# Layer norm's statistics partly on ScalarE, ReLU-squared wholly on ScalarE, and one more feature block ahead of each down projection, in a two-layer decoder trunk

## The chip, the cores and the metric

The kernel runs on one core of one Trainium2 chip. The time is that of one execution on the device, in microseconds (us); less is better. TensorE (PE) multiplies matrices, VectorE (DVE) and ScalarE (ACT) work element by element, GpSimd (POOL) takes a part of the subtractions, and SyncE (SP) issues the transfers. Each engine runs its instructions in the order in which they were written for it.

## The reference, cut to what matters

Two decoder layers over 512 rows of 1024 numbers in fp32. Layer 0 mixes with latent attention and windowed attention, layer 1 with forgetting attention. Each layer is

```
x = LN(alpha * x + mixer(x))                       # "ln1"
x = LN(alpha * x + square(relu(x @ w_up)) @ w_down) # "ln2"; w_up 1024x4096, w_down 4096x1024
x = x + sigmoid(x @ w_gate + b_gate) * (p @ w_proj)
LN(x) = (x - mean) * rsqrt(var + 1e-5) * g + b      # over the 1024 numbers of a row
```

## The kernel before, in words

**Tiling.** The rows are four blocks `tb` of 128. `x[tb][h]` is a tile of 128 rows by 512 columns, `h` being the half of the columns. PE needs its inputs split into a high part and a rest (`split`: ACT copies to the high part, DVE or POOL subtracts it), and each product is three matmuls (`mm3`). The transposed activations are the tiles `xh` and `xl`; `to_X` makes them from `x[tb]`: four transposes by PE for each half, then a split.

**Layer norms.** `out_proj` multiplies half 0 for all blocks and then half 1 block by block; after each bank DVE adds `ALPHA*x` (L1239), and after half 1 of a block `ln1` runs `layer_norm` and `to_X` for it. `down`, the end of the feed-forward part, does the same by block with `ln2` (residual sum L1352). `layer_norm` is DVE work alone: statistics of both halves (L1214), mean and variance (L1216), the square root's inverse by an integer start and three Newton steps on 128x1 columns (L1217, `rsqrt` L631 to L640), and two passes over each half (L1220, L1222).

**Feed-forward.** `up` makes one block of 128 of the 4096 features: 24 matmuls into one bank, then `relu2`, in which ACT takes the ReLU (L1259) and DVE multiplies it by the bank again (L1260), so the bank is free only after DVE. `up_first` makes the first four blocks in halves of 256 rows: the first half needs only row blocks 0 and 1. Features go in groups of four. `forms` turns a group into the seven sums and differences of a fast 2x2 product (splits and subtractions by ACT and DVE); `down_pairs` multiplies them by seven forms of the weights (tiles `wf`, made by `form`) into banks `t`, `mm` and `s`, and DVE adds each bank to `x` (L1330, L1332). PE's order is: one block of the next group, the products of this group, three more blocks.

**Order.** `Plan` lists every operation with an estimated duration and lays them out by engine: each engine takes the ready operation of the lowest number, and buffers come from rings of fixed depth (`DEPTH`; 12 tiles `w`, two for a plain weight, one for a form). That order is then fixed for each engine.

Of the kernel before, what the change touches and what calls it, by code (L numbers as in the profile page):

```python
# [93 lines left out]
def weight_pieces():  # L94
# [337 lines left out]
class Trunk:  # L432
# [194 lines left out]
    def rsqrt(self, y, v, r, w, n=1):  # L627
# [4 lines left out]
        d(lambda e: e.tensor_scalar(hv[:], v(), -0.5, None, ALU.mult), r, [hv])  # L632
        d(lambda e: e.tensor_scalar(y().bitcast(I32), y().bitcast(I32), -1, 0x5F3759DF, ALU.mult, ALU.add), [], [w])
# [573 lines left out]
        return [self.load("u", (P, 512), lambda h=h: self.A["rows"][i:i + 1, 512 * h:512 * h + 512].broadcast_to([P, 512]), name)  # L1207
                for h in range(2)]

    def layer_norm(self, x, g, b):  # L1210

        st, mv, rv = self.small("bn", 12), self.small("mv", 4), self.small("rv", 4)
        for h in range(2):
            self.dve(S, lambda e, h=h: e.bn_stats(st[:, 6 * h:6 * h + 6], x[h][:]), [x[h]], [(st, h)])  # L1214

        self.dve(1, lambda e: e.bn_aggr(mv[:, 0:2], st[:].rearrange("p (a b) -> p a b", a=2)), [st], [mv])  # L1216
        self.dve(1, lambda e: e.tensor_scalar(rv[:, 0:1], mv[:, 1:2], EPS, None, ALU.add), [mv], [(rv, 0)])  # L1217
        self.rsqrt(lambda: rv[:, 1:2], lambda: rv[:, 0:1], [(rv, 0)], (rv, 1))
        for h in range(2):
            self.dve(S + 57, lambda e, h=h: e.scalar_tensor_tensor(x[h][:], x[h][:], mv[:, 0:1], g[h][:], ALU.subtract, ALU.mult),  # L1220
                     [mv, g[h]], [x[h]], port=True)
            self.dve(S + 57, lambda e, h=h: e.scalar_tensor_tensor(x[h][:], x[h][:], rv[:, 1:2], b[h][:], ALU.mult, ALU.add),  # L1222
                     [(rv, 1), b[h]], [x[h]], port=True)

    def out_proj(self, x, order, after):
        xh, xl = self.X
        for h in range(2):
            ws = [self.weights() for _ in range(4)]
            banks = [None] * TB

            def step(tb, i):
                if i == 0:
                    banks[tb] = self.bank()
                ks = (2 * order[i], 2 * order[i] + 1)
                self.natural(banks[tb], 512, ws[i], tb, ks, i == 0, i == 3)
# [99 lines left out]
    def down(self, rl, x, after):  # L1335
# [3 lines left out]
            self.split(S, lambda a=a: a[:], lambda r=r: r[:, 0, :], lambda r=r: r[:, 1, :], [a], [r], psum=False)  # L1339
        ws = [self.weights() for _ in range(4)]  # L1340
        for tb in range(TB):
            ts = slice(tb * P, (tb + 1) * P)
            for h in range(2):
                cs = slice(512 * h, 512 * (h + 1))
                b = self.bank()
                for j in range(4):
                    r, w = rt[j], ws[j]
                    self.mm3(512, lambda b=b: b[:], (lambda r=r, ts=ts: r[:, 0, ts], lambda r=r, ts=ts: r[:, 1, ts]),
                             (lambda w=w, cs=cs: w[0][:, cs], lambda w=w, cs=cs: w[1][:, cs]), j == 0, j == 3,
                             [r] + list(w), [b])  # L1350
# [52 lines left out]
    def run(self):  # L1403
        A = self.A
        for l in range(2):
# [12 lines left out]
            def ln1(tb):  # L1418
                self.layer_norm(x[tb], g1, b1)
# [57 lines left out]
```

## Time and profile before

| | |
|---|---|
| three runs | 1271.53 us median (1270.67 to 1274.31) |
| the profiled execution | 1274.59 us, of which the span of instructions is 1272.8 us |
| busy: PE, DVE, ACT, POOL | 1237.7, 1008.5, 615.4, 503.2 us |
| TensorE's granted clock over the run | 0.995 of full speed |

The profile is of one execution. Its span runs from the first instruction to the last; 1.8 us lie around it. A row of the profile gives an engine, a line of the kernel and a tile; busy time counts an instruction from its start to its end, and neighbours on an engine overlap a little, so the step from one start to the next is shorter than a duration.

### The profile page before, as it was taken

What the parts mean: (1) busy time and instruction counts of PE and PEld (TensorE: products, weight loads), DVE (VectorE), ACT (ScalarE), POOL (GpSimd) and SP (SyncE); (2) the same over time, 40 slices, a digit from 0 to 9 for tenths busy, and PEclk for the clock granted to TensorE, in tenths of its full rate; (3) what the DMA queues carried; (4) which work ended last, traced back from release to release, by engine and by line L of the source; (5) the groups of instructions that cost most, each with busy time, mean ns of one, the idle gap of its engine ahead of it and who ended that gap; (6) DMA issues with size and microseconds to landing.
All of it is one profiled execution on the core that took longest, in us unless ns stands there. A gap on an engine that the chain in (4) does not pass through costs nothing.

```text
span 1272.8 us, 17267 instructions
## 1 busy us (share of the span) xinstructions
PE 1237.7 (97%) x6108; PEld 1044.7 (82%) x6108; DVE 1008.5 (79%) x1847; ACT 615.4 (48%) x1180; POOL 503.2 (40%) x408
## 2 busy tenths in 40 slices
PE   9998999999999999999999999999999999999998
PEld 6887888878888888888898888888788888888877
DVE  5668969799898999595543686878998998897774
ACT  6658852434444344334445697823444444444241
POOL 2445432445454444212213475422455444543110
PEclk9999999999999999999999999999999999999999
DMA  6422523124323222413222412531223242232131
GB/s 202 147 78 79 166 100 114 35 100 134 97 69 133 99 95 88 141 65 136 92 93 91 149 67 92 182 132 51 99 84 115 99 132 85 81 133 94 55 116 50
DMA packets 46791, 132.83 MB, mean 104 GB/s; under 512 B 5984, under 2 KB 8672, under 8 KB 46704
## 3 DMA queue, kind: packets, MB, share of 16 engines
q1 hardware_dynamic: 46704, 131.72, 31.0%
q8 instruction: 48, 0.79, 0.2%
q14 instruction: 39, 0.32, 0.1%
HBM read 126.03 MB, written 4.62 MB: 103 GB/s over the span
## 4 chain that ended last, share of the span: by engine, by line
PE 78%; DVE 13%; ACT 4%; issue 2%; DMA 2%; POOL 1%; SPq 0%; DVEq 0%; ACTq 0%; POOLq 0%
PE mm L512 30%; PE s L512 20%; PE t L512 15%; PE o L512 10%; PE t L523 2%; DVE wl L488 1%; DMA raw<-in_wall_dram 1%; DVE x L1220 1%; ACT t L664 1%; DVE x L1222 1%; DVE t L659 1%; DVE wf L488 1%; DVE xl L503 1%; DVE rl L503 1%; DVE qlo L753 1%
## 5 line engine op out<-in xcount | busy, mean ns | idle before, releaser
L488 POOL TENSOR_TENSOR wl<-raw,wh 128x1024 fp32r<-128x1024 f32 (+4 forms) x78 | 183.4, 2352 | 450.6 <-ACT wh L551 379.8
L551 ACT CAST wh<-raw 128x1024 fp32r<-128x1024 f32 (+5 forms) x150 | 151.8, 1018 | 195.3 <-DMA raw<-in_wall_dram 101.8
L488 POOL TENSOR_TENSOR wf<-raw,wf 128x512 fp32r<-128x512 f32 x84 | 124.5, 1503 | 128.2 <-ACT wf L584 128.2
L512 PE MATMUL mm<-xh,wh 128*128 128x512 f32 (+1 forms) x416 | 163.1, 392 | 1.9 <-DVE k L766 0.8
L512 PE MATMUL mm<-xl,wh 128*128 128x512 f32 (+1 forms) x416 | 160.7, 386 | 1.0 <-DVE xl L503 1.0
L512 PE MATMUL mm<-xh,wl 128*128 128x512 f32 (+1 forms) x416 | 160.3, 385 | 0.0
L584 ACT CAST wf<-raw 128x512 fp32r<-128x512 f32 x168 | 98.8, 619 | 32.0 <-PE t L512 16.6
L488 DVE TENSOR_TENSOR wl<-raw,wh 128x1024 fp32r<-128x1024 f32 (+4 forms) x72 | 95.7, 1329 | 21.1 <-ACT wh L551 18.4
L512 PE MATMUL t<-wf,rh 128*128 128x512 f32 x336 | 103.7, 390 | 0.0
L488 DVE TENSOR_TENSOR wf<-raw,wf 128x512 fp32r<-128x512 f32 x84 | 100.9, 1220 | 0.0
L673 POOL TENSOR_SCALAR t<-t,st 128x256 f32<-128x256 f32 (+3 forms) x128 | 69.4, 562 | 76.1 <-DVE st L670 52.7
L512 PEld LDWEIGHTS mm<-xh,wh 128*128 128x128 f32 x416 | 79.7, 192 | 19.3 <-ACT q L755 2.2
L512 PEld LDWEIGHTS mm<-xl,wh 128*128 128x128 f32 x416 | 79.8, 192 | 15.8 <-DVE xl L503 2.1
L512 PEld LDWEIGHTS mm<-xh,wl 128*128 128x128 f32 x416 | 79.6, 191 | 15.6 <-DVE wl L503 0.4
L512 PE MATMUL mm<-wh,xh 128*128 128x384 f32 (+5 forms) x232 | 82.8, 357 | 6.5 <-DVE qlo L753 2.7
L512 PE MATMUL mm<-wl,xh 128*128 128x384 f32 (+5 forms) x232 | 80.7, 348 | 0.2 <-POOL wl L488 0.2
L512 PE MATMUL mm<-wh,xl 128*128 128x384 f32 (+5 forms) x232 | 80.7, 348 | 0.0
L664 ACT ACTIVATE t<-t,st 128x256 f32<-128x256 f32 (+3 forms) x128 | 68.7, 539 | 13.0 <-DVE st L659 10.8
L512 PEld LDWEIGHTS t<-wf,rh 128*128 128x128 f32 x336 | 62.9, 188 | 13.7 <-DVE x L1330 0.7
L512 PE MATMUL s<-wf,rh 128*128 128x512 f32 x224 | 69.0, 389 | 0.0
L1332 DVE TENSOR_TENSOR x<-x,t 128x512 f32<-128x512 f32 x100 | 65.2, 677 | 1.4 <-PE t L512 1.3
L512 PE MATMUL t<-wf,rl 128*128 128x512 f32 x168 | 65.4, 389 | 0.0
(296 smaller groups left out, 3240.2 us busy)
## 6 DMA issues: line engine op xcount, KB each, us to landing
raw<-in_wall_dram SPq DMA_DIRECT2D x183, 512.0 KB, 3.3
ck<-scratch_c SPq DMA_DIRECT2D x16, 256.0 KB, 4.0
raw<-in_wall_dram SPq DMA_DIRECT2D x9, 384.0 KB, 3.1
x<-in_xT_dram SPq DMA_DIRECT2D x8, 256.0 KB, 5.4
x<-in_xn_dram SPq DMA_DIRECT2D x8, 256.0 KB, 4.9
g<-in_rows_dram SPq DMA_DIRECT2D x8, 256.0 KB, 4.7
b<-in_rows_dram SPq DMA_DIRECT2D x8, 256.0 KB, 6.3
scratch_x<-x SPq DMA_DIRECT2D x8, 256.0 KB, 2.3
```

What stands on the lines that cost most here:

```text
L488: fn = lambda e: e.tensor_tensor(out(), a(), b(), op)
L503: sub = lambda e: e.tensor_tensor(lo(), src(), hi().bitcast(F), ALU.subtract)
L512: return [self.nc.tensor.matmul(o(), a(), b(), start=s, stop=e, **kw) for o, a, b, s, e in prods]
L523: lambda: [self.nc.tensor.transpose(o(), i(), self.ident[:]) for o, i in items],
L551: self.act(w, lambda e: e.copy(hi[:, :w], raw[:, :w]), [raw], [hi])
L584: self.act(512, lambda e: e.copy(t[:, h[0]], src()), [key], [(t, 0)])
L659: return e.tensor_tensor_reduce(t[:, offs[i] + a:offs[i] + z], b[:, c + a:c + z], ad(), -scale, init, ALU.add, ALU.min, nm[:, i:i + 1])
L664: self.act(n, lambda e, i=i, tt=tt: e.activation(tt(), tt(), AF.Exp, bias=nm[:, i:i + 1], scale=-1.0, accum_out=sm[:, i:i + 1]), [(nm, i)] ...
L673: self.pool(0.13 + 1.21e-3 * n, lambda e, i=i, tt=tt: e.tensor_scalar(tt(), tt(), rc[:, i:i + 1], 1.0, ALU.mult, ALU.mult), [rc], [(t, i)])
L753: self.dve(S, lambda e, q2=q2, lo=lo, rs=rs: e.tensor_tensor(lo[rs, :], bank[rs, :], q2[rs, :].bitcast(F), ALU.subtract), [bank, (q2, 0)], ...
L1220: self.dve(S + 57, lambda e, h=h: e.scalar_tensor_tensor(x[h][:], x[h][:], mv[:, 0:1], g[h][:], ALU.subtract, ALU.mult), [mv, g[h]], [x[h] ...
L1332: self.dve(S, lambda e, b=b, xx=xx: e.tensor_tensor(xx[:], xx[:], b[:], ALU.add), [b], [xx])
```

## The change

- The row sum of the residual comes out of the same DVE instruction that adds it (`add_sum`, one column per half in a tile `st`). For `out_proj` ACT multiplies `x` by `ALPHA` ahead of that.
- `layer_norm`: DVE makes the negated mean from the two sums; ACT squares each half less the mean and sums it (bias and accumulator); DVE adds the two sums; ACT takes the square root; DVE takes its reciprocal and one Newton step. The two passes over each half stay.
- `relu2`: the square is an ACT instruction on the tile in SBUF, and DVE has no part in it.
- `ffn`: two blocks of the next group stand ahead of the products of this one, two behind; the weights are stored in that order.

```diff
-            up(range(4 * g + 4, 4 * g + 5) if g < 7 else ())
+            up(range(4 * g + 4, 4 * g + 6) if g < 7 else ())
...
-            up(range(4 * g + 5, 4 * g + 8) if g < 7 else ())
+            up(range(4 * g + 6, 4 * g + 8) if g < 7 else ())
...
+    def add_sum(self, xx, b, st, h):
+        self.dve(S + 26, lambda e: e.tensor_tensor_reduce(xx[:], b[:], xx[:], 1.0, 0.0, ALU.add, ALU.add, st[:, h:h + 1]),
+                 [b], [xx, (st, h)])
...
-    def layer_norm(self, x, g, b):
-        st, mv, rv = self.small("bn", 12), self.small("mv", 4), self.small("rv", 4)
-            self.dve(S, lambda e, h=h: e.bn_stats(st[:, 6 * h:6 * h + 6], x[h][:]), [x[h]], [(st, h)])
-        self.dve(1, lambda e: e.bn_aggr(mv[:, 0:2], st[:].rearrange("p (a b) -> p a b", a=2)), [st], [mv])
-        self.dve(1, lambda e: e.tensor_scalar(rv[:, 0:1], mv[:, 1:2], EPS, None, ALU.add), [mv], [(rv, 0)])
-        self.rsqrt(lambda: rv[:, 1:2], lambda: rv[:, 0:1], [(rv, 0)], (rv, 1))
...
+    def layer_norm(self, x, st, g, b):
+        d(lambda e: e.tensor_scalar(c(nm), st[:, 0:1], st[:, 1:2], -1.0 / D, ALU.add, ALU.mult), [st], [nm], 0.1)
+            self.act(S, lambda e, h=h, junk=junk: e.activation(junk[:], x[h][:], AF.Square, bias=c(nm), accum_out=q[:, h:h + 1]),
+                     [x[h], nm], [junk, (q, h)], aps=2)
...
+        d(lambda e: e.scalar_tensor_tensor(c(v), q[:, 0:1], D * EPS, q[:, 1:2], ALU.add, ALU.add), [q], [v], 0.1)
+        self.act(1, lambda e: e.activation(c(t), c(v), AF.Sqrt, scale=1.0 / D), [v], [t])
+        d(lambda e: e.reciprocal(c(y), c(t)), [t], [y], 0.1)
+        d(lambda e: e.tensor_scalar(c(hv), c(v), -0.5 / D, None, ALU.mult), [v], [hv])
+        d(lambda e: e.tensor_scalar(c(t), c(y), c(y), c(hv), ALU.mult, ALU.mult), [y, hv], [t], 0.19)
+        d(lambda e: e.scalar_tensor_tensor(c(y), c(t), 1.5, c(y), ALU.add, ALU.mult), [t], [y], 0.1)
...
+        for h in range(2):
+            for tb in range(TB):
+                self.act(S, lambda e, xx=x[tb][h]: e.mul(xx[:], xx[:], ALPHA), [], [x[tb][h]])
...
-                    self.dve(S, lambda e: e.scalar_tensor_tensor(xx[:], xx[:], ALPHA, b[:], ALU.mult, ALU.add), [b], [xx])
+                    self.add_sum(xx, b, sums[tb], h)
...
-            rl = [self.up()]
+            rl = [self.up() for _ in range(2)]
             self.down_pairs(g, rt, x)
-            rl += [self.up() for _ in range(3)]
+            rl += [self.up() for _ in range(2)]
...
-        self.dve(n, lambda e: e.scalar_tensor_tensor(rl[:, c0:c1], b[:, c0:c1], 0.0, rl[:, c0:c1], ALU.max, ALU.mult),
-                 [b], [(rl, c0)])
+        self.act(n, lambda e: e.activation(rl[:, c0:c1], rl[:, c0:c1], AF.Square), [], [(rl, c0)])
```

## Rows read from the trace of the kernel before

**Rows 1.** Busy time by stretch of the span: length; then PE, its weight loads (PEld), DVE, ACT and POOL with their instructions; TensorE's granted clock; DMA share and GB/s. 262:534 and 918:1186 are the feed-forward groups of the two layers, 534:582 is ln2 of layer 0.

```profile
262.00:534.00 272.00, 271.92 (x1199) 224.56 (x1198) 242.50 (x312) 117.13 (x193) 124.78 (x76) 1.00 0.32 107
534.00:582.00 48.00, 48.00 (x227) 39.66 (x226) 41.91 (x93) 17.40 (x26) 7.58 (x3) 1.00 0.23 81
...
918.00:1186.00 268.00, 268.00 (x1183) 221.97 (x1183) 237.85 (x307) 117.52 (x193) 122.34 (x73) 1.00 0.32 105
```

**Rows 2.** The same view in steps of 5 us through ln1 of layer 0.

```profile
205.00:210.00 5.00, 5.00 (x28) 4.24 (x27) 5.00 (x18) 1.44 (x2) 0.34 (x1) 1.00 0.00 2
...
215.00:220.00 5.00, 4.53 (x34) 3.92 (x33) 5.00 (x11) 2.38 (x4) 2.52 (x1) 1.00 0.32 107
...
230.00:235.00 5.00, 3.99 (x19) 3.22 (x20) 2.75 (x5) 1.17 (x2) 0.00 (x0) 0.72 0.00 0
```

**Rows 3.** The chain that ended last, in order of time: start, length, what. Layer 0's last halves of `up_first` and one undisturbed `up`, one half's transposes in ln2 of layer 0, the last `up_first` bank of layer 1.

```profile
242.84 2.89 PE s L512 x24
...
278.25 5.44 PE mm L512 x24
...
549.27 0.44 PE t L523 x4
...
894.46 2.89 PE o L512 x24
```

**Rows 4.** PE's instructions in order of time: start, duration, form, and in brackets the idle time before and what ended it. In layer 0 the first transposes of row block 0, the last matmul of `out_proj` and the first transposes of row block 3; then the last matmul of `out_proj` in layer 1.

```profile
208.57 0.60 PE L523 MATMUL s<-ident,x 128*128 128x128 f32 x4
...
213.32 0.39 PE L512 MATMUL s<-wh,xl 128*128 128x512 f32 x1
...
230.79 0.66 PE L523 MATMUL t<-ident,x 128*128 128x128 f32 x4 [1.59 <-DVE x L1222]
...
865.20 0.39 PE L512 MATMUL s<-wh,xl 128*128 128x512 f32 x1
```

**Rows 5.** Who waited for whom on PE over the whole run: us in total, times, the longest.

```profile
PE mm L512 <- DVE rl L1260: 3.4, 2, 1.7
...
PE mm L512 <- DVE x L1352: 0.7, 1, 0.7
PE mm L512 <- ACT pr L1373: 0.7, 1, 0.7
```

**Rows 6.** The chain again, DVE's pieces in ln1 of layer 0, row blocks 0 and 1.

```profile
201.02 0.22 DVE mv L1216
...
201.27 0.15 DVE rv L1217
201.42 0.66 DVE x L1220
202.08 0.06 DVE rv L631
202.14 0.06 DVE nh L632
...
202.78 0.14 DVE rv L633
202.93 0.59 DVE x L1239
203.52 0.19 DVE nt L636
203.71 0.60 DVE bn L1214
204.31 0.06 DVE rv L640
...
207.21 1.33 DVE x L1222 x2
```

**Rows 7.** DVE's and ACT's groups over the run by line and shape: count | busy us, mean ns of one | idle time before, and what ended it.

```profile
L1260 DVE SCALAR_TENSOR_TENSOR rl<-mm,rl 128x512 f32<-128x512 f32 x28 | 19.2, 686 | 10.1 <-ACT rl L1259 9.9
...
L659 DVE CUSTOM_DVE_ANT_0 t<-s,cmask 128x512 f32<-128x512 f32 x8 | 5.4, 681 | 0.0
...
L659 DVE DVE_READ_ACCUMULATOR2_ANT st<- 128x1 f32 x176 | 14.3, 81 | 0.0
...
L670 DVE RECIPROCAL st<-st 128x4 f32<-128x4 f32 x32 | 5.5, 173 | 6.8 <-ACT t L664 6.5
...
L664 ACT ACTIVATE t<-t,st 128x512 f32<-128x512 f32 x24 | 17.3, 719 | 2.6 <-DVE st L659 2.6
...
L664 ACT ACTIVATION_READ_ACCUMULATOR t<-t,st 128x1 f32 x128 | 24.4, 190 | 0.0
...
L668 ACT ACTIVATE st<-st,sinks 128x4 f32<-128x4 f32 x8 | 2.3, 289 | 0.0
...
L502 ACT ACT_TABLE_LOAD x1 | 1.3, 1283 | 0.7 <-PEq L1466 0.7
...
L1119 ACT ACT_TABLE_LOAD x1 | 1.3, 1283 | 0.0
```

**Rows 8.** ACT in order of time: the table load of layer 1 ahead of the logarithm (L1118) and the instruction after it; then ACT's longest idle time in ln1 of layer 0.

```profile
657.18 1.28 ACT L1118 ACT_TABLE_LOAD   x1
658.48 0.64 ACT L1118 ACTIVATE fl<-fw 16x512 f32<-16x512 f32 x1
...
208.53 1.05 ACT L551 CAST wh<-raw 128x1024 fp32r<-128x1024 f32 x1 [10.44 <-PE s L512]
```

More of the change, by code (lines that the diff above doesn't have):

```diff
@@ L625, in to_X, with rsqrt @@
                        lambda ks=ks: xl[:, ks, ts], [b], cells)
-    def rsqrt(self, y, v, r, w, n=1):
+    def rsqrt(self, y, v, r, w, n=1, scale=0):
         t, hv = self.small("nt", n), self.small("nh", n)
@@ L631, in rsqrt @@
         d(lambda e: e.tensor_scalar(y().bitcast(I32), v().bitcast(I32), 1, None, ALU.arith_shift_right), r, [w])
-        d(lambda e: e.tensor_scalar(hv[:], v(), -0.5, None, ALU.mult), r, [hv])
-        d(lambda e: e.tensor_scalar(y().bitcast(I32), y().bitcast(I32), -1, 0x5F3759DF, ALU.mult, ALU.add), [], [w])
+        d(lambda e: e.tensor_scalar(hv[:], v(), -0.5 / 4 ** scale, None, ALU.mult), r, [hv])
+        d(lambda e: e.tensor_scalar(y().bitcast(I32), y().bitcast(I32), -1, 0x5F3759DF + (scale << 23), ALU.mult, ALU.add), [], [w])
         for _ in range(3):
@@ L1208, in row @@
                 for h in range(2)]
-    def layer_norm(self, x, g, b):
-        st, mv, rv = self.small("bn", 12), self.small("mv", 4), self.small("rv", 4)
+    def add_sum(self, xx, b, st, h):
+        self.dve(S + 26, lambda e: e.tensor_tensor_reduce(xx[:], b[:], xx[:], 1.0, 0.0, ALU.add, ALU.add, st[:, h:h + 1]),
+                 [b], [xx, (st, h)])
+    def layer_norm(self, x, st, g, b):
+        nm, q, v, y = (self.small(n, 4) for n in ("nm", "sq", "va", "rs"))
+        c = lambda z: z[:, 0:1]
+        d = lambda fn, r, w, dur=0.07: self.dve(1, fn, r, w, dur=dur)
+        d(lambda e: e.tensor_scalar(c(nm), st[:, 0:1], st[:, 1:2], -1.0 / D, ALU.add, ALU.mult), [st], [nm], 0.1)
@@ L1213, in layer_norm @@
         for h in range(2):
[L1214 to L1218 removed]
+            junk = self.u("junk")
+            self.act(S, lambda e, h=h, junk=junk: e.activation(junk[:], x[h][:], AF.Square, bias=c(nm), accum_out=q[:, h:h + 1]),
+                     [x[h], nm], [junk, (q, h)], aps=2)
@@ L1219, in layer_norm @@
         for h in range(2):
[L1220 to L1223, printed above, removed]
+            self.dve(S + 57, lambda e, h=h: e.scalar_tensor_tensor(x[h][:], x[h][:], c(nm), g[h][:], ALU.add, ALU.mult),
+                     [nm, g[h]], [x[h]], port=True)
@@ new lines, in layer_norm @@
+        d(lambda e: e.scalar_tensor_tensor(c(v), q[:, 0:1], D * EPS, q[:, 1:2], ALU.add, ALU.add), [q], [v], 0.1)
+        hv, t = self.small("hv", 4), self.small("nt", 4)
+        self.act(1, lambda e: e.activation(c(t), c(v), AF.Sqrt, scale=1.0 / D), [v], [t])
+        d(lambda e: e.reciprocal(c(y), c(t)), [t], [y], 0.1)
+        d(lambda e: e.tensor_scalar(c(hv), c(v), -0.5 / D, None, ALU.mult), [v], [hv])
+        d(lambda e: e.tensor_scalar(c(t), c(y), c(y), c(hv), ALU.mult, ALU.mult), [y, hv], [t], 0.19)
@@ L1225, in out_proj @@
+        d(lambda e: e.scalar_tensor_tensor(c(y), c(t), 1.5, c(y), ALU.add, ALU.mult), [t], [y], 0.1)
+        for h in range(2):
+            self.dve(S + 57, lambda e, h=h: e.scalar_tensor_tensor(x[h][:], x[h][:], c(y), b[h][:], ALU.mult, ALU.add),
+                     [y, b[h]], [x[h]], port=True)
     def out_proj(self, x, order, after):
         xh, xl = self.X
+        sums = [self.small("st", 4) for _ in range(TB)]
+        for h in range(2):
+            for tb in range(TB):
+                self.act(S, lambda e, xx=x[tb][h]: e.mul(xx[:], xx[:], ALPHA), [], [x[tb][h]])
@@ L1238, in step @@
                     xx = x[tb][h]
-                    self.dve(S, lambda e: e.scalar_tensor_tensor(xx[:], xx[:], ALPHA, b[:], ALU.mult, ALU.add), [b], [xx])
+                    self.add_sum(xx, b, sums[tb], h)
                     if h == 1:
-                        after(tb)
+                        after(tb, sums[tb])
             steps = [(tb, i) for i in range(4) for tb in range(TB)] if h == 0 else \
@@ L1341, in down @@
         for tb in range(TB):
-            ts = slice(tb * P, (tb + 1) * P)
+            ts, st = slice(tb * P, (tb + 1) * P), self.small("st", 4)
             for h in range(2):
@@ L1350, in down @@
                              [r] + list(w), [b])
-                xx = x[tb][h]
-                self.dve(S, lambda e, b=b, xx=xx: e.tensor_tensor(xx[:], xx[:], b[:], ALU.add), [b], [xx])
-            after(tb)
+                self.add_sum(x[tb][h], b, st, h)
+            after(tb, st)
     def ple_proj(self, l):
@@ L1416, in run, with ln1 @@
             g1, b1 = self.row(l, "g1"), self.row(2 + l, "b1")
-            def ln1(tb):
-                self.layer_norm(x[tb], g1, b1)
+            def ln1(tb, st):
+                self.layer_norm(x[tb], st, g1, b1)
                 self.to_X(x[tb], tb)
@@ L1423, in run, with ln2 @@
             rows = {}
-            def ln2(tb):
+            def ln2(tb, st):
                 if not rows:
                     rows["g"], rows["b"] = self.row(4 + l, "g2"), self.row(6 + l, "b2")
-                self.layer_norm(x[tb], rows["g"], rows["b"])
+                self.layer_norm(x[tb], st, rows["g"], rows["b"])
                 self.to_X(x[tb], tb)
@@ L1446 @@
 DEPTH = {"xh": 1, "xl": 1, "ident": 1, "raw": 2, "w": 12, "t5": 6, "u": 42, "mm": 2, "s": 3, "t": 2, "o": 1,
-         "sm1": 8, "sm4": 16, "sm12": 3, "sm16": 4, "sm64": 1, "sm128": 3, "sm256": 2}
+         "sm1": 8, "sm4": 28, "sm16": 4, "sm64": 1, "sm128": 3, "sm256": 2}
 def build(tc, A, out, scratch):
```

## The prediction

> **What bounds the kernel now.** I read the busy time by stretch first. In the feed-forward groups PE is busy for the whole stretch, 271.92 of 272 us and 268.00 of 268, and a block of 24 matmuls always takes 5.44 us [rows 1, 3]. DVE is busy for 89% there and PE never waits for it, so DVE work taken out of these groups is worth nothing by itself. In ln2 of layer 0 PE is full too, 48.00 of 48 [rows 1]. Then I looked for stretches where PE is not full. In ln1 of layer 0 DVE is busy for 5.00 of 5 us and PE is not (4.53), and right after it the granted clock drops to 0.72, that is, PE has spent part of that step at the lower of its two levels after waiting [rows 2]. So the change can pay only around ln1 of both layers, at the start of their feed-forward parts, and a little in ln2 of layer 1.
>
> What these places cost is the distance between two points less the work between them. In layer 0 the last matmul of `out_proj` starts at 213.32 and its successor could start 0.23 later (5.44/24), at 213.55; `up_first` ends at 242.84 + 2.89 = 245.73 [rows 3, 4]. Between them lie eight half blocks and the transposes of row blocks 1 to 3. A half block without a stall is 2.88 us (2.89 in the row) and a half's transposes 0.44: 8 x 2.88 + 6 x 0.44 = 25.7. The distance is 32.2, so **6.5 us** are lost, of which one wait for L1222 is 1.59 [rows 4]; the rest is in smaller waits and at the lower clock. In layer 1 the same count gives 894.46 + 2.89 - 865.43 = 31.9, less 25.7: **6.2 us** [rows 3, 4]. In the first group of each layer PE waits 1.7 us for L1260 [rows 5]: the bank `mm` of the block that went ahead isn't free until DVE has squared it, and a product needs that bank. Two waits of 0.7 are left in ln2 of layer 1, one for the residual sum L1352, one for ACT's L1373 [rows 5]. In all 6.5 + 6.2 + 3.4 + 1.4 = 17.5 us are to be had.
>
> **The change, part by part.**
>
> *DVE in a norm.* Removed per row block: two L1214 of 0.60, 0.22 for L1216, 0.15 for L1217, 0.06 + 0.06 + 0.14 for L631 to L633, three Newton steps of 0.19 + 0.06 [rows 6]: 2.58 us. Added: two accumulator reads of 0.08, the negated mean and the sum of squares at 0.15 each (as L1217), a reciprocal of 0.17, and 0.06 + 0.19 + 0.06 for the one Newton step [rows 6, 7]: 0.94. The adding instruction itself costs the same: 681 ns in the reducing form with 512 columns, while the step from L1239 to the next is 0.59 and from L1214, of like size, 0.60 [rows 6, 7]. So DVE is relieved of 1.64 us per block, 6.6 per norm. Four of the eight half squares of `up_first` also ran on DVE before row block 3 was done: 4 x 0.34 (half of 686 ns [rows 7]) = 1.4. The relief is 8.0 us where 6.5 are lost, so the last row block can come early enough: PE then needs 2 x 0.88 + 4 x 2.88 = 13.3 us from 213.55 before it wants block 3, that is at about 226.9; its transposes started at 230.79 [rows 4], and 230.79 - 8.0 = 222.8 leaves 4 us for what follows.
>
> *New waits.* DVE must now wait for ACT twice per block. The squares take 719 ns and an accumulator read each; as reads and activations overlap I take 0.73 a half, 1.5 in all. Behind them on DVE stand the two passes with `g`, 2 x 0.66 [rows 6], which need only the mean, so some 0.2 us stays open. The root is 0.29 (a 128x4 activation [rows 7]) with nothing sure to cover it; DVE's reciprocal waits, and behind it whatever the order put there: the next block's sum, `xl` splits, weight subtractions. About 0.4 a block with handovers, from 0 (other work stands between) to 2.1 (nothing does, not even the passes). Ahead of the first root ACT has to load another table: 1.28 us, with the next activation 1.30 after its start [rows 8]. No Sqrt is in the trace of before; the three loads are at the start, for Ln and for the Exp after it [rows 7, 8]. The load lies on block 0's chain, and block 0's transposes start at 208.57, in the middle of PE's `out_proj`, 0.03 us after DVE's second pass ends (207.21 + 1.33) [rows 4, 6]: just in time. As PE runs in order, lateness there stops `out_proj`. I charge 1.28 + 0.4 = 1.7 us to each ln1, from 0 (the order leaves room) to 3.4 (blocks 0 and 1 both late). The later blocks are covered by the relief. In each ln2 the table is still there and I charge 0.4.
>
> The Trainium skill (ScalarE: Activation LUTs, "What ACT_TABLE_LOAD costs") gives about 2.66 us for each switch, load and drain together. Here the load takes 1.28 and no drain shows behind it [rows 8]; by the page's figure the estimate would be 1.4 us later per ln1, 2.8 in all.
>
> *ACT.* Added per layer: 28 squares of 512 and eight of 256 columns, at most 28 x 0.72 + 8 x 0.5 = 24 us, into stretches where ACT is busy 117 of 272 us [rows 1]; per norm 8 x 0.73 plus four roots, 7 us, where it is busy 1.44 and 2.38 of 5 us [rows 2]; eight products with `ALPHA` per layer, 8 x 0.72 = 5.8 at most, where ACT has a gap of 10.44 us at the end of `out_proj` and others before [rows 8]. I cost them at nothing; without the cover, a product that came late would delay a residual sum by its 0.7.
>
> *The bank and the two blocks ahead.* With the square on ACT in SBUF the bank is free after the ReLU, and one more block of 5.44 us stands between `up_first` and the first products. The 1.7 us per layer go: 3.4. The steady groups keep four blocks between two sets of products in either order, so their weights come as before; at the end two blocks instead of three stand before `down`, with the same weights behind them. Nothing for both. Late next in the first group would be the forms of activations and weights, up to the same 1.7 a layer.
>
> *ln2.* Layer 1 gets back the 0.7 of L1352; the one on ACT stays. Layer 0 has nothing to give back.
>
> **Sum.** ln1 of layer 0: 6.5 - 1.7 = 4.8; ln1 of layer 1: 6.2 - 1.7 = 4.5; first groups 3.4; ln2: 0.7 - 0.8 = -0.1. Together 12.6. The profiled execution took 1274.6 us, so 1262.0; it stood 3.1 above the median of 1271.5, so against the median I forecast **1259**.
>
> **The rivals.**
>
> *A, the waits on ACT eat the relief.* If nothing stands between the sum of squares and the reciprocal, and the passes with `g` stand behind both, each block costs 2.1 us of waiting against 1.64 saved. ln1 then stays as it was, less the half squares, and only the first groups gain: 1271.5 - 3.4 = 1268, between 1266 and 1271. For it: DVE is one queue and its order is fixed beforehand. Against: weights and splits of other blocks stand in the same stretch.
>
> *B, the first group turns to its weights.* The two blocks ahead hold four of the 12 `w` tiles, so no form of a weight can be made until `up_first` gives tiles back. The 1.7 us come back as a wait for `wf`: 1259 + 3.4 = 1262. Against: two blocks are 10.9 us for the first forms.
>
> *C, slower: the table is changed to and fro.* If Square or ReLU were not in the table with Sqrt, each block would load twice, 2.6 us, 16 x 2.6 = 41 in the run; DVE's relief covers 16 x 1.64 = 26 of it, and 15 less the 3.4 of the first groups makes 1283. It decides from 1.64 us a block, that is, from the second load on. For it: no row shows Sqrt. Against: Square, ReLU, Exp and Tanh run between the three loads without another [rows 7]. The Trainium skill (ScalarE: Activation LUTs, "Table sets: the hidden batching unit") has sqrt in another set than exp and tanh, with cheap functions as filler in every set; it names ReLU and copy, not Square, and no run here shows it yet.
>
> *D, the change does little:* other operation counts give the attention stages another order, which can cost or gain about what one ln1 does, 5 us: 1264 to 1274.
>
> **How the numbers follow.** The likeliest, 1259 (1254 to 1265), gets 0.58; A 0.20; B 0.10; C 0.06; D 0.06. The low end of the range is nearly all of the 17.5 with no lateness at block 0, plus what one stretch of reordering could add: 1252. The high end, 1270, takes in most of A and D; outside stay C and a tenth of the rest. A measurement tells 0.3%, 3.8 us, from no change, so faster means below 1267.7: the likeliest, B, a quarter of A and a third of D, 0.75. Slower is C and a little of D, 0.08; the same 0.17.
>
> **What would show it.** Right: no L1214 and no L1260; PE's distance from the last matmul of `out_proj` to the end of `up_first` near 26 to 27 us; the granted clock at full through it; no wait of PE for a bank in the first group; four more table loads (one ahead of each ln1, one ahead of each gate); block 0's transposes waiting about 1.7 us. The prediction is wrong if DVE shows long idle time that ends with ACT's root, if PE waits for `wf`, if there are more than seven loads, or if the attention stages change by more than a few us.

## The result, and the profile after

The changed kernel takes 1261.97 us (median; 1261.16 to 1265.41) where the kernel before took 1271.76 beside it (1270.67 to 1274.31): a ratio of 0.9925, 95% interval 0.9902 to 0.9949. The forecast was 1259 us, in a range from 1252 to 1270. The profiled execution took 1265.41 us, its span 1263.6; in the experiments the same code was profiled twice more, with spans of 1261.7 and 1260.3.

DVE is busy for 949.7 us in place of 1008.5, ACT for 687.2 in place of 615.4, PE for 1233.4. The first view is busy time by stretch, columns as in [rows 1]: the feed-forward groups of layer 0, ln2 of layer 0, the groups of layer 1.

```profile
258.00:530.00 272.00, 271.28 (x1195) 223.83 (x1194) 228.96 (x290) 131.72 (x220) 125.94 (x75) 1.00 0.32 105
530.00:578.00 48.00, 48.00 (x227) 39.69 (x226) 34.64 (x72) 25.26 (x48) 9.45 (x6) 1.00 0.29 94
911.00:1179.00 268.00, 268.00 (x1184) 221.82 (x1183) 223.41 (x285) 129.65 (x217) 124.59 (x74) 1.00 0.32 106
```

PE is as full as in [rows 1], and DVE has 14 us less to do in each set of groups: relief that buys nothing there. In ln1 of layer 0, in steps of 5 us as in [rows 2], DVE is no longer full, PE loses 0.9 us in one step, and the granted clock stays at full:

```profile
205.00:210.00 5.00, 5.00 (x28) 4.18 (x27) 4.72 (x12) 2.89 (x7) 0.00 (x0) 1.00 0.00 2
...
225.00:230.00 5.00, 4.09 (x35) 3.88 (x33) 4.93 (x10) 2.83 (x7) 1.31 (x1) 1.00 0.31 105
230.00:235.00 5.00, 5.00 (x43) 5.00 (x44) 2.00 (x3) 1.97 (x4) 0.00 (x0) 1.00 0.34 108
```

PE in order of time, layer 0, as in [rows 4]: the first transposes of row block 0, the last matmul of `out_proj`, the first transposes of row block 3. Then the last matmul of `out_proj` in layer 1.

```profile
207.35 0.60 PE L523 MATMUL s<-ident,x 128*128 128x128 f32 x4
...
217.77 0.39 PE L512 MATMUL s<-wh,xl 128*128 128x512 f32 x1
...
230.00 0.66 PE L523 MATMUL t<-ident,x 128*128 128x128 f32 x4 [0.92 <-DVE x L1237]
...
866.50 0.39 PE L512 MATMUL s<-wh,xl 128*128 128x512 f32 x1
```

The chain, as in [rows 3]: the last bank of `up_first` and the block behind it, layer 0.

```profile
241.16 2.88 PE s L512 x24
244.04 5.47 PE mm L512 x24
```

The prediction's distance in ln1 (from 0.23 us after the start of `out_proj`'s last matmul to the end of `up_first`) is 244.04 - 218.00 = 26.0 us, and 26.0 in layer 1, where the chain has `up_first` end at 892.73. It was 32.2 and 31.9. The transposes of row block 1 now stand ahead of `out_proj`'s end (212.35), so the work in between is 24.8 us instead of 25.7, and 1.2 us are still lost in each layer: the wait for L1237 at row block 3, 0.92 and 0.88, and little else. In the first groups PE waits for nothing. Who waited for whom on PE, the two rows that are left around the change:

```profile
PE t L523 <- DVE x L1237: 1.8, 2, 0.9
...
PE t L512 <- DVE x L1350: 0.7, 1, 0.7
```

A part of what came back in ln1 is TensorE's clock. Before, each ln1 has one stretch at the lower level, 1.2 GHz. In layer 0 it shows in the 0.72 of [rows 2] and in the next step, in layer 1 in these two (the kernel before, columns as in [rows 1]):

```profile
235.00:240.00 5.00, 5.00 (x41) 5.00 (x41) 1.46 (x3) 1.79 (x5) 2.25 (x2) 0.94 0.01 3
...
880.00:885.00 5.00, 3.05 (x17) 2.18 (x17) 4.12 (x11) 1.56 (x3) 0.00 (x0) 0.92 0.00 0
885.00:890.00 5.00, 5.00 (x35) 5.00 (x34) 0.00 (x0) 1.33 (x4) 0.63 (x1) 0.74 0.01 3
```

Some sixteen matmuls of 256 columns start 0.213 us apart there, and 0.120 apart right after it: 1.5 us are lost in each layer. Both times the clock fell behind PE's waits for a norm, the longest of them 1.59 us in either layer [rows 4]. In the changed kernel PE waits 0.92 and 0.88 us there, and the clock stays at 2.4 GHz.

**Where the time went.** PE starts 6108 instructions in every one of these traces. So the n-th can be set against the n-th of the kernel before (up to each place named below the same shapes have run, in whatever order), and what its lag grows by between two places is what a stage cost or gave. The stages end in the trace of before at 125.6, 189.1 (end of attention, layer 0), 242.2 (ln1), 273.5 (first group), 808.6, 843.7 (end of attention, layer 1), 895.3 (ln1), 932.4 (first group) and 1267.9 us. In us, minus is a gain, worked out from the start times:

```
                 start  att0   ln1  1st g.  to att1  att1   ln1  1st g.  rest | sum
changed            2.5   1.1  -5.2   -2.6     1.5     3.1  -5.0   -2.6   -2.0 |  -9.2
e_same             1.6   1.1  -5.2   -2.6     0.4     3.1  -5.0   -2.6   -2.0 | -11.2
f_same            -0.8   1.0  -5.2   -2.6     1.1     3.2  -5.0   -2.6   -1.6 | -12.5
e_relu_only        1.4   0.0  -2.1   -0.5     0.3    -0.1  -2.4   -0.5    0.0 |  -3.9
e_order_only      -0.4   0.0  -2.4   -2.6     0.5    -0.1  -3.0   -2.6    0.0 | -10.5
e_relu_order       1.7   0.0  -3.5   -2.6     0.6    -0.1  -3.5   -2.6    1.4 |  -8.4
e_norm_only        0.3   1.0  -4.2    0.0     0.0     3.3  -4.0    0.3   -2.1 |  -5.4
e_root_dve         0.5   1.0  -2.8   -2.6     0.9     3.1  -2.9   -2.6   -1.3 |  -6.6
e_alpha_twice     -1.0   1.4  -5.2   -2.6     1.2     5.4  -4.8   -2.6   -1.9 | -10.0
e_fold_alpha       0.0   0.0  -4.8   -2.6     1.1     0.0  -5.0   -2.6   -2.0 | -15.9
f_fold            -1.2  -0.1  -4.9   -2.6     0.2    -0.1  -5.0   -2.6   -0.9 | -17.0
f_fold_apart      -1.7  -0.1  -4.9   -2.6     1.7     0.0  -5.5   -2.6   -0.9 | -16.6
```

The first three rows are the same code: the start varies by 3 us from execution to execution and the feed-forward parts by 1, the stages around the change by 0.1. So stages are compared below by this table, and whole kernels by their medians.

### The profile page after: what moved, and what is told of

Same layout as the page of the kernel before. It is cut to its first block, busy times and chain, and to the rows that moved or that the text cites. A ratio compares the mean times of both kernels' runs of the same rounds, so it can differ in the third digit from the quotient of the medians.

```text
span 1263.6 us, 17349 instructions
## 1 busy us (share of the span) xinstructions
PE 1233.4 (98%) x6108; PEld 1042.6 (83%) x6108; DVE 949.7 (75%) x1695; ACT 687.2 (54%) x1352; POOL 505.2 (40%) x408
## 4 chain that ended last, share of the span: by engine, by line
PE 81%; ACT 8%; DVE 6%; issue 2%; DMA 2%; POOL 1%; SPq 0%; ACTq 0%; DVEq 0%; POOLq 0%
PE mm L512 31%; PE s L512 21%; PE t L512 16%; PE o L512 10%; ACT t L664 2%; PE t L523 2%; ACT wh L551 1%; DVE wl L488 1%; DMA raw<-in_wall_dram 1%; ACT pth L502 1%; DVE qlo L753 1%; ACT q L755 1%; ACT q L752 1%; DVE t L659 1%; POOL wl L488 0%
## 5 line engine op out<-in xcount | busy, mean ns | idle before, releaser
L488 DVE TENSOR_TENSOR wl<-raw,wh 128x1024 fp32r<-128x1024 f32 (+4 forms) x72 | 102.5, 1423 | 47.8 <-ACT wh L551 38.3
L488 DVE TENSOR_TENSOR wf<-raw,wf 128x512 fp32r<-128x512 f32 x84 | 77.4, 936 | 17.4 <-ACT wf L584 17.1
```

The lines of the kernel that those rows point to most:

```text
L488: fn = lambda e: e.tensor_tensor(out(), a(), b(), op)
```

## The experiments

**Three parts, alone and together.** The changed kernel again (e_same); the kernel before with the square on ACT alone, with the two blocks ahead alone, and with both (e_relu_order); and the changed kernel with both undone, which leaves the new norms and the `ALPHA` passes (e_norm_only).

```diff
 e_relu_only
-        self.dve(n, lambda e: e.scalar_tensor_tensor(rl[:, c0:c1], b[:, c0:c1], 0.0, rl[:, c0:c1], ALU.max, ALU.mult),
-                 [b], [(rl, c0)])
+        self.act(n, lambda e: e.activation(rl[:, c0:c1], rl[:, c0:c1], AF.Square), [], [(rl, c0)])
 e_order_only
-            rl = [self.up()]
+            rl = [self.up() for _ in range(2)]
...
-            rl += [self.up() for _ in range(3)]
+            rl += [self.up() for _ in range(2)]
```

In e_order_only the weights are stored in that order too.

> The changed kernel again, beside the three variants of it that follow. All theories: 1262 us, 9 to 10 below the kernel before. In its profile the stretch from the last matmul of out_proj to the end of up_first should again be 26 to 27 us in both layers; if the 0.9 us wait of PE for L1350 at 478 us and the 2.5 us lost in the first 15 us are of that one execution, they are missing here; if they belong to the program, they are here again.

> The kernel before with one part of the change: relu2's square on ACT. Theory (the bank is free after the ReLU, so the first group's wait of 1.7 us goes in each layer; DVE loses 1.4 us of half squares ahead of row block 3 in each ln1): 3.4 + 2.8 = 6 below the kernel before on the same chip, 0.995. Rival (the wait is removed by the second block ahead of the products, not by the bank): the wait stays, and 0.998.

> The kernel before with one part of the change: two blocks ahead of the products of a group and two behind. Theory: the second block uses bank o, so the bank mm of the first has 5.4 us more until a product needs it, and DVE's late square no longer stops PE: 3.4 below the kernel before, 0.997, nothing in ln1. Rival (the 12 weight tiles come short in the first group): PE waits for wf there and the time is that of the kernel before.

> Both parts together on the kernel before, with its old norms. Theory: they take away the same wait, so the two gains don't add: 6 below, as with relu2 alone, 0.995. Rival (they take away different waits): 9 below, 0.993.

> The changed kernel with the old relu2 and the old order of blocks, that is, the new norms and the passes with ALPHA alone. Theory: ln1 gives back some 5 us in each layer, ln2 of layer 1 gives 2, the passes with ALPHA take 4, and the first group's wait of 1.7 stays: 8 below the kernel before, 0.994. Rival (the norms bring nothing without the half squares off DVE): 0.998 or above, with PE still waiting for L1237 at row block 3 by more than 2 us.

e_same was timed beside a median of 1274.56 us of the kernel before, the other four beside 1273.97.

| | median us (range) | ratio to before, interval |
|---|---|---|
| e_same | 1262.38 (1261.27 to 1263.65) | 0.9903, 0.9884 to 0.9923 |
| e_relu_only | 1268.01 (1267.61 to 1270.78) | 0.9961, 0.9947 to 0.9975 |
| e_order_only | 1265.58 (1263.71 to 1268.43) | 0.9938, 0.9920 to 0.9956 |
| e_relu_order | 1262.83 (1261.54 to 1266.16) | 0.9916, 0.9900 to 0.9931 |
| e_norm_only | 1269.43 (1267.09 to 1271.32) | 0.9961, 0.9949 to 0.9974 |

e_same came at the time expected. e_relu_only gained the 6 us expected by its median, though not at the places expected; the other three missed: e_order_only gained 8.4 where 3.4 were expected, e_relu_order 11.1 where 6 or 9 were, e_norm_only 4.5 where 8 were.

The order alone takes away the whole loss of the first group, 2.6 us a layer, and the square on ACT alone a fifth of it. Who waited for whom on PE in e_relu_only, and then the wait that e_norm_only keeps (L1279 is its DVE square):

```profile
PE t L512 <- DVE x L1329: 2.3, 2, 1.2
```

```profile
PE mm L512 <- DVE rl L1279: 3.4, 2, 1.7
```

With the square on ACT, the bank `mm` is no longer late, but the first residual sum (L1329) is: DVE was behind with everything there. In the kernel before the square L1260 itself started late, at 257.59, in a queue that had the forms ahead of it and no idle time from 247.8 to 258.0. The second block ahead gives DVE the time to catch up; without it a bank that comes free sooner only shows the next late thing.

The order gives 2.4 and 3.0 us in ln1 as well, which the prediction had not counted. DVE's groups by line and shape between 213 and 230 us show how, the kernel before first and e_order_only second:

```profile
L488 DVE TENSOR_TENSOR wf<-raw,wf 128x512 fp32r<-128x512 f32 x2 | 1.4, 680 | 0.0
L488 DVE TENSOR_TENSOR raw<-raw,raw 128x512 f32<-128x512 f32 x2 | 1.3, 658 | 0.0
...
L488 DVE TENSOR_TENSOR wl<-raw,wh 128x1024 fp32r<-128x1024 f32 x1 | 1.2, 1215 | 0.0
```

```profile
L488 DVE TENSOR_TENSOR wl<-raw,wh 128x1024 fp32r<-128x1024 f32 x2 | 2.4, 1191 | 0.0
```

Before, DVE made weight forms (`wf`, and the sums `raw` for them), 2.7 us of work for the products to come, in the middle of the norms on which PE waited; in their place stands one more split of a plain weight, 1.2 us. With two blocks ahead, the four of `up_first` and these two hold all 12 `w` tiles, and no form can be begun until `up_first` gives tiles back. Of the 2.4 and 3.0 us, 1.5 each are the clock, which no longer falls.

The parts don't add up: by their medians the three alone gain 6.0, 8.4 and 4.5 us, 18.9 in sum, and all together 12.2. Most of the difference is the clock. Each part by itself is enough to keep it at full through ln1 of both layers, and the 1.5 us per layer can be gained only once; counted three times they are 6 us too many. The windows of layer 0 in e_relu_only, e_order_only and e_norm_only, in this order (in 850:905, layer 1, the clock is 1.00 in all three as well):

```profile
195.00:250.00 55.00, 52.69 (x332) 46.57 (x331) 48.48 (x101) 24.30 (x45) 18.61 (x10) 1.00 0.25 79
```

```profile
195.00:250.00 55.00, 52.73 (x333) 46.79 (x332) 49.52 (x108) 20.54 (x38) 18.09 (x10) 1.00 0.24 79
```

```profile
195.00:250.00 55.00, 54.09 (x342) 48.26 (x341) 44.07 (x85) 28.99 (x60) 18.93 (x12) 1.00 0.21 68
```

On top of the other two parts the new norms bring little. By the stage table they add 1.7 and 1.5 us in ln1 and 2.0 in the last column, and the `ALPHA` passes that came with them take 4.2. The ratios of e_relu_order, with the old norms, and of e_same can't be told apart by their intervals; only without the passes (f_fold below, 0.9852 to 0.9883) do the norms pay.

**The same tiles without the order.** The kernel before with one size changed:

```diff
-DEPTH = {"xh": 1, "xl": 1, "ident": 1, "raw": 2, "w": 12, "t5": 6, "u": 42, "mm": 2, "s": 3, "t": 2, "o": 1,
+DEPTH = {"xh": 1, "xl": 1, "ident": 1, "raw": 2, "w": 10, "t5": 6, "u": 42, "mm": 2, "s": 3, "t": 2, "o": 1,
```

> The kernel before with 10 w tiles in place of 12, old norms, old relu2, one block ahead. It is not meant to be fast (weights are made later everywhere). Theory: the two blocks ahead give 2.4 to 3 us in ln1 because they take the last w tiles, so that no weight form is made by DVE there; with 10 tiles and one block ahead the five plain blocks hold all tiles too, and ln1's loss falls from 6.4 to some 4 us without the order being touched. Rival: the gain is due to the order itself; then the loss stays near 6.4 us.

It took 1308.74 us (one run), and most of the loss lies outside ln1 (23.4 us between the first group of layer 0 and the end of attention in layer 1). The distance in ln1 falls from 31.9 to 29.5 us in layer 1, where e_order_only has 28.9, as the theory has it. In layer 0 it stays at 31.8 (before 32.1; starts of the first and last matmul), which taken alone is the rival's number. DVE makes no form there either, but in order of time DVE and POOL show something else:

```profile
219.06 3.58 DVE L1222 SCALAR_TENSOR_TENSOR x<-x,rv,b 128x512 f32<-128x512 f32 x2
```

```profile
219.04 2.38 POOL L488 TENSOR_TENSOR wl<-raw,wh 128x1024 fp32r<-128x1024 f32 x1 [15.31 <-ACT wh L551]
```

Two passes that take 1.33 us together in [rows 6] take 3.58, the first of them 2.92: it starts with a subtraction on POOL and ends after it. PE waits for the first of them, and then its clock falls:

```profile
222.03 0.44 PE L523 MATMUL mm<-ident,x 128*128 128x128 f32 x2 [1.21 <-DVE x L1222]
```

```profile
225.00:230.00 5.00, 5.00 (x33) 5.00 (x33) 5.00 (x17) 0.93 (x1) 2.38 (x1) 0.70 0.44 132
```

Less this wait and the 1.5 us that the lower level costs, the distance would be some 29 us, near the 29.7 of e_order_only; this is an estimate. So layer 1 bears the tiles out, and layer 0 only if the subtraction is to blame, which wasn't tried by itself.

**The square root.** The changed kernel with the root made on DVE, by an integer start and three Newton steps.

```diff
-        self.act(1, lambda e: e.activation(c(t), c(v), AF.Sqrt, scale=1.0 / D), [v], [t])
-        d(lambda e: e.reciprocal(c(y), c(t)), [t], [y], 0.1)
+        d(lambda e: e.tensor_scalar(c(y).bitcast(I32), c(v).bitcast(I32), 1, None, ALU.arith_shift_right), [v], [y])
...
-        d(lambda e: e.tensor_scalar(c(t), c(y), c(y), c(hv), ALU.mult, ALU.mult), [y, hv], [t], 0.19)
-        d(lambda e: e.scalar_tensor_tensor(c(y), c(t), 1.5, c(y), ALU.add, ALU.mult), [t], [y], 0.1)
+        d(lambda e: e.tensor_scalar(c(y).bitcast(I32), c(y).bitcast(I32), -1, 0x5F3759DF + (5 << 23), ALU.mult, ALU.add), [], [y])
+        for _ in range(3):
+            d(lambda e: e.tensor_scalar(c(t), c(y), c(y), c(hv), ALU.mult, ALU.mult), [y, hv], [t], 0.19)
+            d(lambda e: e.scalar_tensor_tensor(c(y), c(t), 1.5, c(y), ALU.add, ALU.mult), [t], [y], 0.1)
```

> The root goes back to DVE (integer start and three Newton steps, as before); ACT keeps the squares, and there is no Sqrt and no table load for it: three loads in the run instead of seven. DVE has about 0.45 us more per row block. The prediction's term (the table load makes ln1 1.7 us late in each layer): 1259, 3 below the changed kernel. Rival (the load runs while DVE is at its passes with g and costs nothing): 1262, or up to 1 us more for the longer chain on DVE.

1267.44 us (1267.00 to 1269.15), ratio 0.9946 (0.9929 to 0.9963), against 1262.38 for e_same on the same chip: slower than either theory had it. In ln1 it loses 2.4 and 2.1 us against the changed kernel. In ln2 of layer 1 it loses 0.6: counted from the place that PE reaches at 1181.8 us in the trace of before, it gains 1.5 us to the end, where every trace with the root on ACT gains 2.0 to 2.1. So the table load and the wait for ACT are cheaper than the Newton steps on DVE: counted from the end of attention, block 0's transposes start 2.0 and 1.4 us later with the Newton steps. The changed kernel's table loads, by line, and its first norm, ACT and then DVE in order of time, show why:

```profile
L1231 ACT ACT_TABLE_LOAD x2 | 2.6, 1283 | 0.0
L1416 ACT ACT_TABLE_LOAD x2 | 2.6, 1283 | 0.0
L502 ACT ACT_TABLE_LOAD x1 | 1.3, 1283 | 0.7 <-PEq L1483 0.7
L1118 ACT ACT_TABLE_LOAD x1 | 1.3, 1283 | 0.0
L1119 ACT ACT_TABLE_LOAD x1 | 1.3, 1283 | 0.0
```

```profile
201.69 0.72 ACT L1223 ACTIVATE junk<-x,nm 128x512 f32<-128x512 f32 x1 [2.15 <-DVE nm L1220]
...
202.41 0.71 ACT L1223 ACTIVATE junk<-x,nm 128x512 f32<-128x512 f32 x1
...
203.23 1.28 ACT L1231 ACT_TABLE_LOAD   x1
204.52 0.20 ACT L1231 ACTIVATE nt<-va 128x1 f32<-128x1 f32 x1
```

```profile
202.54 1.46 DVE L1226 SCALAR_TENSOR_TENSOR x<-x,nm,g 128x512 f32<-128x512 f32 x2 [0.88 <-ACT junk L1223]
203.91 0.15 DVE L1228 SCALAR_TENSOR_TENSOR va<-sq 128x1 f32<-128x1 f32 x1
...
204.76 0.16 DVE L1232 RECIPROCAL rs<-nt 128x1 f32<-128x1 f32 x1 [0.50 <-ACT nt L1231]
```

The passes with `g` write into `x`, which ACT's squares read, so they wait for the squares (0.88 us of idle DVE) and then run while ACT loads the table. DVE waits 0.50 us for the root, and PE not at all: no bracket at 207.35.

**The passes with ALPHA.** Twice the passes (each by the root of `ALPHA`), and none: the softmax weights are multiplied by 1/`ALPHA` in the instruction of POOL that normalises them anyway, `x` is added as it is, and ln1 takes its epsilon over `ALPHA` squared.

```diff
 e_alpha_twice
-        for h in range(2):
+        for h in (0, 0, 1, 1):
             for tb in range(TB):
-                self.act(S, lambda e, xx=x[tb][h]: e.mul(xx[:], xx[:], ALPHA), [], [x[tb][h]])
+                self.act(S, lambda e, xx=x[tb][h]: e.mul(xx[:], xx[:], ALPHA ** 0.5), [], [x[tb][h]])
...
 e_fold_alpha, f_fold
-            self.pool(0.13 + 1.21e-3 * n, lambda e, i=i, tt=tt: e.tensor_scalar(tt(), tt(), rc[:, i:i + 1], 1.0, ALU.mult, ALU.mult),
+            self.pool(0.13 + 1.21e-3 * n, lambda e, i=i, tt=tt: e.tensor_scalar(tt(), tt(), rc[:, i:i + 1], 1.0 / ALPHA, ALU.mult, ALU.mult),
...
-        for h in range(2):
-            for tb in range(TB):
-                self.act(S, lambda e, xx=x[tb][h]: e.mul(xx[:], xx[:], ALPHA), [], [x[tb][h]])
...
-                self.layer_norm(x[tb], st, g1, b1)
+                self.layer_norm(x[tb], st, g1, b1, EPS / ALPHA ** 2)
```

> Each pass with ALPHA is made twice, by the root of ALPHA each time: 32 passes instead of 16, the output is the same. Theory (the passes cost what they take from ACT in a full stretch, 0.25 us each on average): 1266, 4 above the changed kernel, at the end of the attention stages, most of it in layer 1. Rival (order, not ACT's time): 1262 give or take 2.

> No pass with ALPHA on ACT at all: the softmax weights are multiplied by 1/ALPHA in the instruction that divides them by their sum, so that out_proj gives its result over ALPHA, x is added as it is, and ln1 takes EPS/ALPHA^2; the output is the same. Theory (the 16 passes with ALPHA stand in the full stretch of ACT at the end of attention and cost about 1 us in layer 0 and 3 us in layer 1): 1258 us, 4 below the changed kernel, and PE's waits for q (L755) and for ptl (L503) of about 1 us each near 810 to 816 us are gone. Rival (the attention stages lost it because other operation counts gave PE another order): 1262 give or take 2, and waits of like size stand elsewhere in the same stretch.

> The changed kernel once more, beside which the next two are read. 1261 to 1263 us; ratio to the kernel before 0.990 to 0.993.

> No ALPHA passes, as in e_fold_alpha: its trace was 4.8 us shorter than that of the changed kernel, its median 1.5 us lower. If the passes cost what the traces show in the two attention tails (1.1 and 3.1 us), the median stands 3 to 5 us below f_same. If what the passes delay there is made up by something that the profiled executions don't show, it stands 0 to 2 us below.

e_alpha_twice took 1265.52 us (1263.65 to 1267.99) and e_fold_alpha 1260.85 (1258.71 to 1261.82), beside 1262.38 for e_same. That left it open whether the 4.8 us between the spans of e_same and e_fold_alpha (1261.7, 1256.9) were real, as the medians lay only 1.5 apart. A second pair of runs settled it: f_same 1262.03 (1261.23 to 1265.21; 0.9903, 0.9886 to 0.9920), f_fold 1257.72 (1257.61 to 1258.21; 0.9867, 0.9852 to 0.9883), 4.3 apart, and 4.4 in the spans (1260.3, 1255.9).

The stage table says where. The end of attention in layer 1 costs 0.0 us without the passes, 3.1 with them and 5.4 with twice as many; in layer 0 some 1.0 us (1.4 with twice as many) is there in every kernel with passes and in none without. ACT is full there: the changed kernel's windows in layer 1 (columns as in [rows 1]), its last passes, and PE's waits:

```profile
810.00:815.00 5.00, 4.88 (x34) 4.20 (x32) 3.44 (x16) 4.93 (x14) 0.10 (x1) 1.00 0.00 0
815.00:820.00 5.00, 3.88 (x23) 2.89 (x21) 4.47 (x19) 4.97 (x13) 2.05 (x4) 1.00 0.01 3
```

```profile
810.55 1.67 ACT L1245 ACTIVATE x<-x 128x512 f32<-128x512 f32 x3
...
816.04 1.16 ACT L1245 ACTIVATE x<-x 128x512 f32<-128x512 f32 x2
```

```profile
809.51 0.50 PE L512 MATMUL s<-k,q 128*128 128x512 f32 x1 [0.99 <-ACT q L755]
816.45 0.44 PE L523 MATMUL t<-ident,t 128*128 128x128 f32 x2 [1.09 <-DVE ptl L503]
823.05 0.50 PE L512 MATMUL o<-pth,V 128*128 128x512 f32 x1 [0.77 <-DVE oto L717]
```

In f_fold one wait is left in this stretch, the kernel before's own:

```profile
808.22 0.47 PE L512 MATMUL s<-k,q 128*128 128x512 f32 x1 [0.83 <-DVE st L659]
```

The passes stand in ACT's queue among the copies and exponentials of the last heads. Two of the three waits are put down to DVE, but DVE itself had waited for ACT's `pth` just ahead of both, 0.43 us at 815.70 and 0.30 at 821.59.

**The passes with g apart.** f_fold, with these passes written into tiles of their own.

```diff
+        z = [self.u("z") for _ in range(2)]
         for h in range(2):
-            self.dve(S + 57, lambda e, h=h: e.scalar_tensor_tensor(x[h][:], x[h][:], c(nm), g[h][:], ALU.add, ALU.mult),
-                     [nm, g[h]], [x[h]], port=True)
+            self.dve(S + 57, lambda e, h=h: e.scalar_tensor_tensor(z[h][:], x[h][:], c(nm), g[h][:], ALU.add, ALU.mult),
+                     [x[h], nm, g[h]], [z[h]], port=True)
...
```

The passes with `b` then read `z` and write `x`.

> f_fold, and the passes with g write into tiles of their own, so that they need the mean alone and not ACT's two squares, as the prediction had it. If DVE's idle time behind the squares (0.88 us at the first row block) is what is left of ln1's loss, ln1 gives back 0.5 to 1 us per layer and the median falls by 1 to 2 against f_fold. If the passes then run ahead of the squares and leave the table load and the root uncovered, block 0's transposes come late: the 1.7 us of the prediction appear, and the median rises by up to 3.

1258.03 us (1256.99 to 1258.61), ratio 0.9868 (0.9849 to 0.9887): no difference from f_fold. The passes do start without ACT, 0.04 us after the mean. PE's distance in ln1 shrinks by 0.6 and 1.1 us (by 0.0 and 0.5 in the stage table), and the feed-forward part of layer 0 takes 1.5 back. DVE, and who waited on PE:

```profile
198.55 0.20 DVE L1220 TENSOR_SCALAR nm<-st 128x1 f32<-128x1 f32 x1
198.79 1.42 DVE L1227 SCALAR_TENSOR_TENSOR z<-x,nm,g 128x512 f32<-128x512 f32 x2
```

```profile
PE t L512 <- DVE x L1348: 1.5, 2, 0.7
```

Such a wait for a residual sum comes and goes by itself (0.7 in the changed kernel's profile above, none in that of e_same), so it isn't shown that the edit caused it. What is shown is that PE hardly waited at block 0, apart or not: 0.17 us in layer 1 of f_fold_apart, and nothing elsewhere.

## Why the prediction was right, and where it was not

The forecast gain of 12.6 us was met within 3.4 by all three traces (9.2, 11.2, 12.5), and 1259 was 3 below the median. Its terms were not: gains of 17.4 us stand against a loss of 4.2 that it had at nothing. Two errors of 4 to 5 us cancelled, and that the total came out is luck.

**ln1: 4.8 and 4.5 forecast, 5.2 and 5.0 measured.** The count of the loss held: the distance is 26.0, the clock is full, and there is no L1214. Two steps failed, in opposite directions. One is "I charge 1.28 + 0.4 = 1.7 us to each ln1": block 0's transposes waited 0. Of its two bounds, 0 was right, though not for want of lateness. The load is on the chain, but the passes with `g`, which by the prediction "need only the mean", wait for both squares and so come to lie just over it. By the Trainium skill (ScalarE: Activation LUTs, "What ACT_TABLE_LOAD costs") 2.66 us would have been due; the trace doesn't bear this out here, as the load took 1.28 and the root started 1.29 after the load's start.

The other is "230.79 - 8.0 = 222.8 leaves 4 us". Counted from the end of attention, row block 3's transposes came 4.3 us sooner (3.9 in layer 1), not 8.0, though DVE was relieved of more than that. The windows between the two in layer 0, before and changed (DVE's busy time stands third, after PE and PEld):

```profile
189.07:230.79 41.72, 38.85 (x226) 33.50 (x224) 40.27 (x94) 12.04 (x18) 9.71 (x4) 1.00 0.26 89
```

```profile
192.62:230.01 37.39, 36.47 (x214) 32.02 (x212) 30.92 (x67) 19.12 (x39) 7.27 (x3) 1.00 0.30 99
```

DVE has 9.4 us less to do, and is idle for 6.5 us in place of 1.4. Of these, 3.3 us end with ACT's `wh` for a weight subtraction, 1.4 with ACT's first squares and root, and 1.1 with PE's banks. Relief of an engine isn't an earlier end where it then waits for others.

What is left, 1.2 us, is at row block 3, where 4 us of room had been seen. The 0.9 us wait there has a cause that no term had: the sum of two columns in that norm (L1228) takes 2.38 us while POOL subtracts, and 0.15 in the other row blocks. DVE, then POOL:

```profile
223.94 2.38 DVE L1228 SCALAR_TENSOR_TENSOR va<-sq 128x1 f32<-128x1 f32 x1
```

```profile
223.87 2.44 POOL L488 TENSOR_TENSOR wl<-raw,wh 128x1024 fp32r<-128x1024 f32 x1 [5.67 <-ACT wh L551]
```

The seven traces that have new norms with the root on ACT, the square on ACT and the new order hold 14 such norms. In nine, L1228 takes 2.4 us and PE waits 0.88 to 0.92 for row block 3; in five, it takes 0.15 and PE waits 0.00.

**First groups: 3.4 forecast, 5.2 measured.** The wait of 1.7 us [rows 5] is only the part of the loss that one bracket shows; counted from start to start PE lost 2.6. And "the bank `mm` ... isn't free until DVE has squared it" was true but not the cause: DVE was behind. The square on ACT by itself would have brought 1.0 in both layers, the order by itself brings all.

**ln2: -0.1 forecast, 2.0 measured in layer 1.** Both waits of [rows 5] are gone, that for ACT's L1373 too, which "stays" by the prediction. The norms did this: e_relu_only and e_order_only have 0.0 there, e_norm_only 2.1. The 0.4 charged for the root doesn't show.

**ALPHA passes: 0 forecast, 4.2 measured.** This is the term that failed most. The cover that the prediction named, a gap of 10.44 us at the end of `out_proj` [rows 8], exists, but the passes don't run there. They need only `x`, and the order puts them among the last heads, at 150 to 172 and at 801 to 817 us; in layer 1 ACT is busy for 4.93 and 4.97 of 5 us there. A gap covers only what is queued into it. Without the passes the kernel is 4.3 us faster.

**Rivals.** A: DVE's idle time ending with ACT's squares and roots is 3.5 + 1.0 = 4.5 us over 16 blocks in the whole run, 0.3 a block, not 2.1. The two rows are

```profile
L1226 DVE SCALAR_TENSOR_TENSOR x<-x,nm,g 128x512 f32<-128x512 f32 x32 | 23.3, 748 | 3.5 <-ACT junk L1223 3.5
...
L1232 DVE RECIPROCAL rs<-nt 128x1 f32<-128x1 f32 x16 | 2.5, 156 | 1.3 <-ACT nt L1231 1.0
```

But waits on ACT of another kind, those for `wh` above, did take a good part of the relief in ln1. B: no wait for `wf`; the full tiles that spoke for B turned out to be a gain. C: seven loads, as forecast, none for Square or ReLU between the roots. The Trainium skill (ScalarE: Activation LUTs, "Table sets: the hidden batching unit") keeps sqrt in another set than exp, with cheap functions in every set. The trace agrees, with one load ahead of each ln1 (the first at 203.23), and Square ran here ahead of that load and behind it without one of its own. D named the right place, the attention stages, and about the right price, but a wrong cause: it is the added passes, not another order.

## What to carry to other kernels

Work on an engine that is idle on average is free only at the place in its queue where it will run, so look at that stretch, not at the nearest gap; better still, fold a scaling into an instruction that is there. A wait for a bank or tile that ends with a full engine says that the engine is behind: freeing the bank shows the next late thing, while reordering so that the engine has less to do just then (here, by holding back weight forms until the norms are through) removes the loss. When several parts of a change relieve the same engine in the same stretch, measure each alone before adding up their gains: a loss that goes as a whole, as that at the lower clock does here, can be gained only once. And work taken from an engine comes out as an earlier end only where the engine then has its inputs; look for what it would wait for next.

## What the runs showed of the hardware

A DVE instruction can take many times its length when POOL is at work: 2.38 us for 0.15 in the sum L1228 above, which starts 0.07 us after POOL's subtraction and ends with it. In f_fold a pass L1237 of 0.75 us takes 2.9: it begins at 209.6, POOL subtracts from 209.32 to 211.95, the pass ends at 212.50. ln1 of layer 0 is 0.8 us longer in f_fold (26.8 between the starts of the two matmuls, 26.0 in the changed kernel), but this pass doesn't explain it, as the changed kernel loses as much at L1228.

Over the whole run this is much. In the changed kernel 148 of DVE's 1695 instructions are more than 0.4 us longer than the shortest of the same line and shape, 158 us in all, and POOL is at work during each of them. By this estimate a sixth of DVE's busy time, 949.7 us, is waiting for POOL, which busy time doesn't show; in the kernel before it is 159 us of 1008.5. None of the experiments took POOL's work away.

The Trainium skill (SBUF — State Buffer, "Who interferes with whom") states such a lock: a DVE instruction with two inputs in SBUF and a POOL instruction that reads SBUF lock each other out for a whole instruction, and the one that issues first goes first. The traces agree, with 2.38 us for 0.15; the prediction had left POOL out.

The root of a 128x1 column took 0.20 us on ACT, with 0.29 taken from a 128x4 exponential, and a table load of 1.28 us cost PE nothing where DVE had 1.46 us of other work to do meanwhile.
